# Two moves in an attention phase: half of the stacks' transfers to ScalarE's queue, and the adaptive sums at twice the pace

## The chip, the cores and the metric

The kernel runs on one core of a Trainium2 chip. Its time is the device time of one execution in microseconds. Five engines work side by side, each on its own queue in order: TensorE (PE, with its weight loads shown as PEld), VectorE (DVE), ScalarE (ACT), GpSimd (POOL) and SyncE (SP), which here does nothing but issue transfers. A transfer is issued by an instruction in the queue of an engine (SPq or ACTq in the rows) and is then carried out by the core's 16 DMA engines.

## The reference

Two layers over 512 positions of width 1024. Each layer has a mixer and a gated convolution MLP, each behind an RMS norm that is scaled and shifted by a vector `mod = silu(c) @ w_ada[l] + b_ada[l]` of 6 x 1024 numbers.

```python
def reference(x, c, ...):
    for l in range(DEPTH):
        mod = jax.nn.silu(c) @ w_ada[l] + b_ada[l]
        sh_a, sc_a, gt_a, sh_f, sc_f, gt_f = [...split(mod, 6)]
        h = rms_norm(x, g_attn[l]) * (1.0 + sc_a) + sh_a
        x = x + gt_a * hybrid_mixer(h, ...)
        h = rms_norm(x, g_ffn[l]) * (1.0 + sc_f) + sh_f
        x = x + gt_f * conv_glu_ffn(h, ...)
    return rms_norm(x, g_final)
```

The mixer projects `h` to queries, keys and values of 16 heads and joins three kinds of attention: 4 differential heads (two softmaxes subtracted), 6 dilated heads (three sliding windows with strides), and 6 neighbourhood heads, in which a position of the 8 x 64 grid sees 8 rows and 16 columns around it, with a bias per offset. Their outputs go through `w_out`.

## The kernel before, in words

Everything is fp32 made of two reduced parts: each operand is split in `hi` and `lo`, and each product is three matmuls (L487 to L489, or L760 to L762 for values). Weights come in units of up to 512 KB: `emit_raw` (L333) issues the load into one of four `raw` buffers, `emit_split` casts it to `hi` on ScalarE (L355) and subtracts on VectorE or GpSimd to get `lo` (L357).

The numbers of `mod` are made by 96 **adaptive sums**. `ada_step` (L406) takes one 512 KB piece of `w_ada` from a `raw` buffer, multiplies it with `silu(c)` and adds up on VectorE (L416), and then issues the load of the next piece on SP's queue (`ada_load`, L403). So one piece is loaded ahead, and it takes one of the four `raw` buffers that the weights use too. Sixteen sums are made before the first projection, 24 in the attention phase of layer 0, and the other 56 in its MLP. Layer 1 makes none.

`attention_phase` writes out the order of the work by hand. A loop makes one pass after another (`nst` counts them). In a pass the generator `proj()` emits a piece of the projections, `ck.step()` emits the stages of earlier heads that are due, a stack may be emitted, then an adaptive sum may be, and then at most one new attention step. Step `si` counts 16 differential steps (0 to 15), 24 dilated ones (16 to 39; `NDB` is 40) and 12 of the neighbourhood heads (40 to 51). A credit that grows by 1 a pass, up to 0.5, pays for them: 2 for a differential step, 1.5 for a dilated and 1.7 for a neighbourhood step. The order is the same in both layers but for the sums.

In layer 0 a sum is emitted in each fourth pass from step 10 on. What is left of the 24 when the loop ends is emitted right behind it (L1202), ahead of the output projection, its norm and the MLP.

A **stack** is the arrangement of one pair of heads' keys and queries that lets one matmul multiply `hi` and `lo` together. For neighbourhood pairs `na_stack` (L833) copies from the four tiles `natc` to the tiles `ks`, `qs` and `ql`: 12 transfers of 128 KB, all in SBUF, four lines of code (L841, L842, L844, L845). There are three such stacks in each layer, emitted at steps 32, 40 and 44. The tiles `ks`, `qs` and `ql` have two buffers each, so each stack waits for the last score matmul of the stack two before. Between the first and the second stack the values of the neighbourhood heads go to DRAM and come back in another arrangement, in 4 + 4 transfers of 384 KB (`scv<-va`, L868; `va<-scv`, L871).

On the other side of the loop, a dilated step is: score matmuls (L1036, L1037), a masked maximum on VectorE (L1040), exponential (L1045) and scaling (L1050) on ScalarE, transposes on TensorE (L909), the cast of these to `ph` on ScalarE (L913) and the subtraction to `pl` on VectorE (L917), and the product with the values (L930, L932). A neighbourhood step goes the same way (L1078, L1089, L1101, L1107, L1116, L1118, L1122, L1133). The transposes write PSUM tiles `pt`, of which there are two.

Of the kernel before, what the change touches and what calls it, by code (L numbers as in the profile page):

```python
# [176 lines left out]
def build(ctx, tc, a):  # L177
    nc = tc.nc
    V, A, G, PE, SY = nc.vector, nc.scalar, nc.gpsimd, nc.tensor, nc.sync
# [212 lines left out]
    ada_st = {"n": 0}  # L392
# [13 lines left out]
    def ada_step():  # L406
        if ada_st["n"] >= len(ada_list):
            return
        if not ada_raw:
            ada_load()  # L410
        l, j = ada_list[ada_st["n"]]
        cv = cx if ada_st["n"] < 16 else cb
        r = ada_raw.pop(0)
        ada_st["n"] += 1
        junk = tmp((128, D), BF16)
        V.tensor_tensor_reduce(out=junk, in0=r, in1=cv, op0=ALU.mult, op1=ALU.add, scale=1.0,  # L416
                               scalar=par[:, OFF_B + l * 48 + j:OFF_B + l * 48 + j + 1],
                               accum_out=mod[l][:, j:j + 1])
        g, k = divmod(j, 8)
        if g in (1, 4):  # L420
            o = 0 if g == 1 else 8
            base = OFF_GA if g == 1 else OFF_GF
            g = par[:, base + l * 8 + k:base + l * 8 + k + 1]
            A.activation(out=gsc[l][:, o + k:o + k + 1], in_=mod[l][:, j:j + 1], func=AF.Identity, scale=g, bias=g)
        if ada_st["n"] >= 16 or ada_st["n"] + len(ada_raw) < 16 and l == 0:
            ada_load()
# [213 lines left out]
    def attention_phase(l, gen, fest):  # L640
# [8 lines left out]
        def at(shape, dt, tag, bufs):  # L649
            return ap.tile(list(shape), dt, tag=tag, bufs=bufs, name=f"{tag}{uid()}")  # L650

        def mark(lag, *keys):
            ck.after(lag, lambda: ready.update(keys))
# [179 lines left out]
        def na_stack(p):  # L833
            qh, ql, kh, kl = [t.bitcast(F32) for t in natc[p]]
            K = at([128, 2, S], F32R, "ks", 2)
            Q = at([128, 2, S], F32R, "qs", 2)
            L = at([128, 2, S], F32R, "ql", 2)
            Kf, Qf, Lf = K.bitcast(F32), Q.bitcast(F32), L.bitcast(F32)
            for i in range(2):
                rows = slice(64 * i, 64 * i + 64)  # L840
                SY.dma_start(Kf[0:64, i], kh[rows])  # L841
                SY.dma_start(Kf[64:128, i], kl[rows])  # L842
                for half in range(2):
                    SY.dma_start(Qf[64 * half:64 * half + 64, i], qh[rows])  # L844
                    SY.dma_start(Lf[64 * half:64 * half + 64, i], ql[rows])  # L845
            av["nat"] += 4
            stk["c", p] = (K, Q, L)
            mark(2, ("c", p))
# [211 lines left out]
        def nab_load(hd):  # L1060
            b = at([128, 384], F32, "nab", 2)
            SY.dma_start(b, a["nab"][l, hd])
            nab[hd] = b
# [90 lines left out]
        NDB = 4 * HD + 4 * HB  # L1154
# [17 lines left out]
        for p, at_step in enumerate((NDB - 8, NDB, NDB + 4)):  # L1172
            stacks.append((("natc", p), at_step, lambda p=p: na_stack(p)))
# [6 lines left out]
        credit, si, alive, nst = 0.0, 0, True, 0  # L1180
        while alive or si < len(steps) or ck.heap:
            if alive and next(pg, "end") == "end":
                alive = False
            nst += 1
            assert nst < 2000, (si, av, ready)
            ck.step()
            if stacks and stacks[0][0] in ready and si >= stacks[0][1]:
                stacks.pop(0)[2]()
            if si >= NDB - 8 and not nab:
                nab_load(0)  # L1190
                nab_load(1)
            if l == 0 and ada_st["n"] < 40 and nst % 4 == 0 and si >= 10:
                ada_step()
            credit = min(credit + 1.0, 0.5)
            if si < len(steps) and not ck.held:
                per, need, keys, fn = steps[si]
                if credit >= 0 and all(k in ready for k in keys) and all(av[t] >= n for t, n in need.items()):
                    fn()
                    credit -= per
                    si += 1  # L1200
# [174 lines left out]
    for l in range(DEPTH):  # L1375
        oT = attention_phase(l, rb0, fest)
        norm, rb0, fest = ffn_phase(l, oT)
# [64 lines left out]
```

## Time and profile before

| what | value |
|---|---|
| median of 3 runs | 1357.06 us (1354.73 to 1357.70) |
| profiled execution, its own time | 1349.55 us |
| its span | 1347.8 us |
| TensorE busy | 1285.7 us, 95% of the span |
| VectorE busy | 849.0 us, 63% |
| ScalarE busy | 639.8 us, 47% |
| GpSimd busy | 240.0 us, 18% |
| transfers issued from SP's queue | q1, 203.72 MB |
| transfers issued from ScalarE's queue | q10, 2.39 MB |

The profile is of one execution and was faster than the median of the timed runs. Issuing a transfer and waiting for a semaphore are not counted as busy time of an engine.

### The profile page before, as it was taken

What the parts mean: (1) busy time and instruction counts of PE and PEld (TensorE: products, weight loads), DVE (VectorE), ACT (ScalarE), POOL (GpSimd) and SP (SyncE); (2) the same over time, 40 slices, a digit from 0 to 9 for tenths busy, and PEclk for the clock granted to TensorE, in tenths of its full rate; (3) what the DMA queues carried; (4) which work ended last, traced back from release to release, by engine and by line L of the source; (5) the groups of instructions that cost most, each with busy time, mean ns of one, the idle gap of its engine ahead of it and who ended that gap; (6) DMA issues with size and microseconds to landing.
All of it is one profiled execution on the core that took longest, in us unless ns stands there. A gap on an engine that the chain in (4) does not pass through costs nothing.

```text
span 1347.8 us, 18449 instructions
## 1 busy us (share of the span) xinstructions
PE 1285.7 (95%) x6836; PEld 1102.7 (82%) x6836; DVE 849.0 (63%) x1534; ACT 639.8 (47%) x1150; POOL 240.0 (18%) x163
## 2 busy tenths in 40 slices
PE   5988899899999999999999989999999999999997
PEld 4877698778988888888899868987898888888886
DVE  5659777788676566656674786576775434443443
ACT  4546688665533233323342667887554313331331
POOL 2644522133000000000124344212400000000002
PEclk9999999998999999999999999999999999999999
DMA  9676667853466656665524755472433332333211
GB/s 361 232 207 168 187 199 220 233 161 118 148 204 187 201 175 187 199 191 168 173 77 132 189 156 167 121 212 81 125 118 102 94 94 94 94 94 99 86 36 63
DMA packets 75001, 207.28 MB, mean 154 GB/s; under 512 B 8608, under 2 KB 12576, under 8 KB 74784
## 3 DMA queue, kind: packets, MB, share of 16 engines
q1 hardware_dynamic: 74048, 203.72, 50.4%
q10 hardware_dynamic: 864, 2.39, 0.5%
q8 instruction: 54, 0.88, 0.3%
q14 instruction: 35, 0.29, 0.1%
HBM read 180.91 MB, written 15.73 MB: 146 GB/s over the span
## 4 chain that ended last, share of the span: by engine, by line
PE 72%; DMA 9%; DVE 7%; POOL 4%; issue 4%; ACT 3%; SPq 1%; POOLq 0%; DVEq 0%; ACTq 0%
PE pr L489 9%; PE pr L488 9%; PE pr L487 9%; PE s L488 5%; PE s L487 5%; PE s L489 5%; PE pt L488 4%; PE pt L489 4%; PE pt L487 4%; PE o L488 2%; PE o L489 2%; PE o L487 2%; PE pt L909 2%; DMA raw<-w 1%; PE pr L567 1%
## 5 line engine op out<-in xcount | busy, mean ns | idle before, releaser
L355 ACT CAST whi<-raw 128x1024 fp32r<-128x1024 f32 (+2 forms) x136 | 128.1, 943 | 229.6 <-PE pr L489 78.2
L357 POOL TENSOR_TENSOR wlo<-raw,whi 128x768 fp32r<-128x768 f32 (+2 forms) x58 | 115.0, 1988 | 299.4 <-ACT whi L355 275.4
L448 POOL TENSOR_TENSOR tmp<-tmp,tmp 128x256 f32<-128x256 f32 (+1 forms) x38 | 37.0, 976 | 714.3 <-ACT tmp L446 713.5
L357 DVE TENSOR_TENSOR wlo<-raw,whi 128x1024 fp32r<-128x1024 f32 (+1 forms) x78 | 90.8, 1164 | 101.4 <-ACT whi L355 100.6
L416 DVE CUSTOM_DVE_ANT_0 tmp<-raw,cb,par 128x1024 bf16<-128x1024 f32 x80 | 109.4, 1368 | 52.7 <-DMA raw<-w_ada 52.3
L355 ACT CAST fhi<-raw 128x1024 fp32r<-128x1024 f32 (+1 forms) x76 | 74.6, 985 | 130.6 <-PE pr L489 52.8
L357 DVE TENSOR_TENSOR flo<-raw,fhi 128x1024 fp32r<-128x1024 f32 (+1 forms) x74 | 86.9, 1175 | 56.8 <-ACT fhi L355 56.0
L487 PE MATMUL pr<-h,whi 128*128 128x512 f32 (+1 forms) x300 | 113.2, 378 | 0.4 <-DVE tmp L669 0.4
L489 PE MATMUL pr<-h,whi 128*128 128x512 f32 (+1 forms) x300 | 111.5, 372 | 0.4 <-DVE h L483 0.4
L488 PE MATMUL pr<-h,wlo 128*128 128x512 f32 (+1 forms) x300 | 111.7, 372 | 0.0
L487 PE MATMUL pr<-h,fhi 128*128 128x512 f32 (+1 forms) x244 | 86.8, 358 | 0.1
L488 PE MATMUL pr<-h,flo 128*128 128x512 f32 (+1 forms) x244 | 86.5, 356 | 0.0
L489 PE MATMUL pr<-h,fhi 128*128 128x512 f32 (+1 forms) x244 | 85.8, 358 | 0.3 <-DVE h L483 0.3
L917 DVE TENSOR_TENSOR pl<-pt,ph 128x512 fp32r<-128x512 f32 x80 | 54.6, 685 | 18.0 <-ACT ph L913 17.7
L1267 ACT ACTIVATE tmp<-tmp 128x512 f32<-128x512 f32 x44 | 27.6, 631 | 77.7 <-DVE tmp L1262 77.7
L489 PEld LDWEIGHTS pr<-h,whi 128*128 128x128 f32 x300 | 56.7, 189 | 9.5 <-DVE h L483 0.6
L487 PEld LDWEIGHTS pr<-h,whi 128*128 128x128 f32 x300 | 56.8, 189 | 8.9 <-DVE tmp L669 0.7
L488 PEld LDWEIGHTS pr<-h,wlo 128*128 128x128 f32 x300 | 56.9, 190 | 8.7 <-POOL wlo L357 0.6
L913 ACT CAST ph<-pt 128x512 fp32r<-128x512 f32 x80 | 46.5, 582 | 26.2 <-PE pt L909 25.9
L1003 DVE TENSOR_REDUCE sm<-s 128x1 f32<-128x512 f32 x64 | 42.9, 681 | 25.3 <-PE s L1001 25.0
L909 PE MATMUL pt<-cst,tmp 128*128 128x128 f32 x320 | 48.7, 275 | 9.9 <-DVE tmp L1019 7.0
L909 PEld LDWEIGHTS pt<-cst,tmp 128*128 128x128 f32 x320 | 37.7, 140 | 19.8 <-issue 5.9
(287 smaller groups left out, 3704.9 us busy)
## 6 DMA issues: line engine op xcount, KB each, us to landing
raw<-w SPq DMA_DIRECT2D x132, 512.0 KB
raw<-w_ada SPq DMA_DIRECT2D x80, 512.0 KB
raw<-w SPq DMA_DIRECT2D x64, 384.0 KB
araw<-w_ada SPq DMA_DIRECT2D x16, 512.0 KB
raw<-w SPq DMA_DIRECT2D x16, 320.0 KB
graw<-w SPq DMA_DIRECT2D x8, 384.0 KB
scr0b<-nat SPq DMA_DIRECT2D x12, 256.0 KB
qs<-nat SPq DMA_DIRECT2D x24, 128.0 KB
```

Of the source, the lines that this page charges most:

```text
L355: A.copy(hi, r)
L357: (G if on_pool else V).tensor_tensor(out=lo, in0=r, in1=hi.bitcast(F32), op=ALU.subtract)
L416: V.tensor_tensor_reduce(out=junk, in0=r, in1=cv, op0=ALU.mult, op1=ALU.add, scale=1.0, scalar=par[:, OFF_B + l * 48 + j:OFF_B + l * 48 + ...
L448: self.last = self.eng.tensor_tensor(out=self.sq[0][:, sl], in0=self.sq[0][:, sl], in1=self.sq[m][:, sl], op=ALU.add)
L487: PE.matmul(out, wh, hh, start=first, stop=False)
L488: PE.matmul(out, wl, hh, start=False, stop=False)
L489: return PE.matmul(out, wh, hl, start=False, stop=last)
L909: PE.transpose(pt[:, kt], P[:, kt * 128:kt * 128 + 128], ident)
L913: A.copy(st["ph", half][:, :, sl], pt)
L917: V.tensor_tensor(out=st["pl", half][:, :, sl], in0=st["pt", qb], in1=st["ph", half][:, :, sl].bitcast(F32), op=ALU.subtract)
L1003: V.tensor_reduce(out=nm[:, m:m + 1], in_=s, axis=AX.X, op=ALU.max, negate=True)
L1267: A.activation(out=t, in_=t, func=AF.Silu)
```

## The change

In `na_stack` the six transfers of the pair's second head are issued from ScalarE's queue instead of SP's. The adaptive sums of layer 0's attention are emitted in each second pass instead of each fourth, from step 10 on, and only while `si` is under `NDB - 9`, which is 31. The loop behind the attention, which emits what is left of the 24, stays as it was.

```diff
             for i in range(2):
                 rows = slice(64 * i, 64 * i + 64)
-                SY.dma_start(Kf[0:64, i], kh[rows])
-                SY.dma_start(Kf[64:128, i], kl[rows])
+                E = A if i else SY
+                E.dma_start(Kf[0:64, i], kh[rows])
+                E.dma_start(Kf[64:128, i], kl[rows])
                 for half in range(2):
-                    SY.dma_start(Qf[64 * half:64 * half + 64, i], qh[rows])
-                    SY.dma_start(Lf[64 * half:64 * half + 64, i], ql[rows])
+                    E.dma_start(Qf[64 * half:64 * half + 64, i], qh[rows])
+                    E.dma_start(Lf[64 * half:64 * half + 64, i], ql[rows])
...
-            if l == 0 and ada_st["n"] < 40 and nst % 4 == 0 and si >= 10:
+            if l == 0 and nst % 2 == 0 and 10 <= si < NDB - 9 and ada_st["n"] < 40:
                 ada_step()
```

## Rows read from the trace of the kernel before

**Rows 1.** The page: busy time by engine; a group's busy us, mean ns, idle before.

```profile
PE 1285.7 (95%) x6836; PEld 1102.7 (82%) x6836; DVE 849.0 (63%) x1534; ACT 639.8 (47%) x1150; POOL 240.0 (18%) x163
...
L917 DVE TENSOR_TENSOR pl<-pt,ph 128x512 fp32r<-128x512 f32 x80 | 54.6, 685 | 18.0 <-ACT ph L913 17.7
```

**Rows 2.** Waits of TensorE, 200 to 350 us: total, times, longest.

```profile
PE s L1078 <- issue: 4.1, 1, 4.1
```

**Rows 3.** SP's queue in order of time, stacks of layer 1: start, duration.

```profile
862.07 0.51 SPq L844 DMA_DIRECT2D qs<-nat  x1
...
869.35 0.47 SPq L845 DMA_DIRECT2D ql<-nat  x1
...
881.11 2.73 SPq L871 DMA_DIRECT2D va<-scv  x4
886.27 0.52 SPq L844 DMA_DIRECT2D qs<-nat  x1
...
889.77 0.46 SPq L845 DMA_DIRECT2D ql<-nat  x1
893.94 0.46 SPq L841 DMA_DIRECT2D ks<-nat  x1
896.57 0.46 SPq L842 DMA_DIRECT2D ks<-nat  x1
...
899.36 0.59 SPq L845 DMA_DIRECT2D ql<-nat  x1
```

**Rows 4.** SP's queue, second stack of layer 0: first and last issue of twelve.

```profile
227.28 0.52 SPq L841 DMA_DIRECT2D ks<-nat  x1
...
242.42 0.60 SPq L845 DMA_DIRECT2D ql<-nat  x1
```

**Rows 5.** Waits of SP's queue, whole span (first row) and 860 to 915 us.

```profile
SPq L333 <- DMA rope<-rope: 8.6, 1, 8.6
...
SPq L841 <- DMA va<-scv: 3.7, 1, 3.7
```

**Rows 6.** ScalarE and its queue in order of time, layer 0's start and layer 1.

```profile
40.06 0.82 ACT L540 ACTIVATE h<-xt,mod,gsc 128x512 fp32r<-128x512 f32 x1
40.07 0.34 ACTq L236 DMA_DIRECT2D rope<-rope  x1
...
889.74 0.58 ACT L913 CAST ph<-pt 128x512 fp32r<-128x512 f32 x1
```

**Rows 7.** TensorE in order of time, layer 1's second stack.

```profile
893.73 0.60 PE L909 MATMUL pt<-cst,tmp 128*128 128x128 f32 x4
```

**Rows 8.** Busy time by stretch: length, engines (instructions), clock, DMA share, GB/s.

```profile
125.00:151.60 26.60, 24.35 (x134) 20.33 (x132) 23.73 (x44) 15.55 (x32) 14.78 (x8) 1.00 0.64 174
151.60:202.40 50.80, 48.58 (x278) 42.45 (x279) 37.78 (x91) 38.43 (x80) 17.52 (x10) 1.00 0.68 204
...
232.50:291.80 59.30, 53.59 (x304) 44.50 (x302) 47.06 (x137) 43.64 (x113) 13.58 (x8) 0.97 0.70 193
291.80:322.20 30.40, 25.55 (x164) 23.44 (x163) 22.67 (x36) 14.24 (x27) 14.90 (x14) 0.89 0.53 173
...
891.80:946.80 55.00, 52.49 (x304) 45.07 (x302) 39.34 (x121) 42.33 (x109) 13.06 (x8) 0.97 0.48 129
946.80:972.10 25.30, 23.58 (x163) 21.72 (x163) 17.72 (x29) 14.39 (x26) 14.25 (x14) 0.93 0.40 125
```

**Rows 9.** VectorE in order of time, five of the attention's 24 sums.

```profile
124.96 1.28 DVE L416 CUSTOM_DVE_ANT_0 tmp<-raw,cb,par 128x1024 bf16<-128x1024 f32 x1
...
198.71 1.26 DVE L416 CUSTOM_DVE_ANT_0 tmp<-raw,cb,par 128x1024 bf16<-128x1024 f32 x1
...
247.08 1.29 DVE L416 CUSTOM_DVE_ANT_0 tmp<-raw,cb,par 128x1024 bf16<-128x1024 f32 x1 [5.54 <-DMA raw<-w_ada]
...
293.11 1.85 DVE L416 CUSTOM_DVE_ANT_0 tmp<-raw,cb,par 128x1024 bf16<-128x1024 f32 x1 [0.70 <-DMA raw<-w_ada]
...
297.94 1.27 DVE L416 CUSTOM_DVE_ANT_0 tmp<-raw,cb,par 128x1024 bf16<-128x1024 f32 x1
```

## The prediction

> **What bounds the kernel now.** I read the page's engine shares first. TensorE is busy for 95% of the span [rows 1], so a change pays only where it fills a gap of TensorE, and costs wherever it opens one. Second, TensorE's waits in the stretch where both edits work. The largest is 4.1 us before a score matmul [rows 2], the eight others are 2.2 us or less, and none names a transfer. So no stack comes late for TensorE, and the stacks' speed is worth nothing by itself. Third, SP's queue in order of time, for what the stacks wait for and how long they take to issue. Fourth, the order of ScalarE and TensorE beside the same stacks, for how much slack ScalarE has. Fifth, busy time by stretch, layer 0 beside layer 1: the same matmuls (304 and 304, 164 and 163), but only layer 0 has adaptive sums. From the first neighbourhood score matmul to the last product with the values layer 0 takes 59.3 us and layer 1 55.0, and from there to the second norm 30.4 and 25.3 [rows 8]. The difference, 4.3 + 5.1 = 9.4 us, is what the sums cost in these stretches now.
>
> **The stacks.** Nothing is added or taken away; 6 of 12 issues move from SP to ScalarE, in three stacks of two layers, 36 issues in all. On SP one issue takes its turn every 0.64 us or so: the first stack of layer 1 runs from 862.07 to 869.82 us, almost without a stop [rows 3]. SP gains 36 x 0.64 = 23 us that nothing on TensorE waits for, so that gain counts as nothing. At most the next weight load or bias load, queued behind the stack, goes out 3.8 us sooner.
>
> *What a moved issue brings along.* The second stack shows it. Its first five issues go out from 886.27 on, and then the sixth starts at 889.77, the seventh at 893.94 and the eighth at 896.57 [rows 3]. They wait for `va<-scv` [rows 5], although `ks<-nat` neither reads nor writes what that transfer moves. Counting issues back from the sixth, seventh and eighth gives the second, third and fourth of the four `va<-scv` in each case: eight places. So a transfer is issued only when the one eight places earlier has landed. That this count runs across queues is seen at the start: a weight load on SP waited 8.6 us for the table `rope`, which ScalarE's queue had issued and which the load doesn't touch [rows 5, 6]. So I take it that ScalarE's issues will hold such places too. In the order of the code they are the seventh to twelfth of a stack. In the second stack the seventh and eighth then wait for the third and fourth `va<-scv`, and the ninth to twelfth for SP's first four of the same stack. On SP such a wait blocks only loads. On ScalarE it blocks, in order, all that stands behind it: casts of weights (L355), the cast of a projection (L820), exponentials (L1045), scalings (L1050), casts of the transposes (L913). TensorE's transposes wait for those, and VectorE's `pl` too.
>
> *Second stack.* ScalarE would reach its six issues at about 886.3, when SP reached the stack, since both wait for the same score matmul, and be through when the twelfth is out: 899.36 + 0.59 = 899.95. It is held 13.7 us. How long does TensorE go on? Its transposes at 893.73 need a `pt` buffer, which the cast L913 of 889.74 to 890.32 and a subtraction of 0.69 us on VectorE free [rows 1, 6, 7]: slack 893.73 - 890.32 - 0.69 = 2.7 us. Loss 13.7 - 2.7 = 11.0 us, in each layer: 22. In layer 0 the stack took 227.28 to 243.02, 15.7 us [rows 4], partly behind loads of sums that will be gone there, so I keep 13.7. At 95% busy [rows 1] TensorE has next to no idle time in which to win that back.
>
> *First and third stacks.* There is no such row in the way; ScalarE is held for its own six issues at least, 6 x 0.64 = 3.8 us, and at most for the whole stack of before, 7.75 us [rows 3]. The ninth must wait until the first has landed. I take 5.2 between the two, less the same slack of 2.7: 2.5 a stack, and 10 for the four.
>
> Stacks together: 22 + 10 = 32 us. Below: nothing, if an issue costs ScalarE no time, as `rope`'s went out at 40.07 while L540 ran from 40.06 [rows 6]. Issue time alone would give 6 x (3.8 - 2.7) = 6.6. Above: (15.7 - 2.7) + 11.0 + 4 x (7.75 - 2.7) = 44.
>
> The Trainium skill, DMA: Bandwidth & Descriptors, section "Issuing engines are not separate DMA queues", says that transfers issued from different engines end on the same 16 DMA engines and that a second issuing engine only saves issue time. By that rule the stacks' edit could give back no more than SP's 23 us, which the rows show to be off the path; it would stand at 0 in the sum, and the sum at 5 us. The rule says nothing of a cost on the engine that issues, which is where the rows put it.
>
> **The sums.** Of before's 24, nine are emitted up to step 31, from 124.96 to 198.71 us [rows 9]: passes 32 to 64. A pass is (198.71 - 124.96) / 32 = 2.3 us. At each second pass from 30 to 64 that is 18. The window then shuts, so six are left, and they go to the loop behind the attention, which emitted three before. So they aren't all ahead of the neighbourhood heads.
>
> - Differential steps (125 to 151.6 us): seven sums instead of three. A sum is 1.28 us and 0.08 for the readout, 4 x 1.36 = 5.4 us more. VectorE is busy 23.73 of 26.6 there [rows 8], so at least 5.4 - 2.9 = 2.5 doesn't fit: 2.5 to 5.4, I take 3.
> - Dilated steps (151.6 to 202.4): eleven instead of six, 6.8 us more, in 13.0 us of idle VectorE [rows 8]. What is late is a load: one piece ahead and a sum each 4.6 us, while a load that SP reached late held VectorE for 5.54 us [rows 9]. 0 to 6.8; I take 2.
> - Neighbourhood steps: eight sums gone, with the 5.54 us wait. It can give back what layer 0 is behind layer 1, 4.3 us; I take 4, and nothing is the other end.
> - Behind the attention: four sums started after 291.8 and cost 5.1 us, 1.3 each; now there are six, none with its load ahead but the first. Two more at 1.3 are 2.6. Above, three more in the loop at the spacing of 293.11 to 297.94 [rows 9], 4.8 each, are 14.5, with the weight loads of the MLP queued behind them on SP. I take 4, near the measured price.
>
> Sums together: 3 + 2 - 4 + 4 = +5 us, from -2 (2.5 + 0 - 4.3 + 0) to +27 (5.4 + 6.8 + 0 + 14.5).
>
> **Sum.** 32 + 5 = 37 us, on the profiled execution's 1349.55 us (span 1347.8): 1386.6. The median of the runs shown lies 7.5 us higher, so 1357.06 + 37 = 1394 us.
>
> **The rivals.**
> *Issue time alone.* ScalarE's issues land in its queue where the places eight back are long free, or count for ScalarE alone. For it: the six of a stack need not follow SP's in the final order. Against it: the 8.6 us across the queues. 6.6 + 5 = +12: 1369 us.
> *Faster.* The same place, ScalarE's queue: if it is held for less than the 2.7 us of slack at each stack, the stacks cost nothing, and the sums' removal gives what layer 0 is behind layer 1, 9.4 us: 1348 us. For it: the issue under L540 [rows 6], and idle VectorE among the dilated steps to take the sums. Against it: six times 0.64 is already over 2.7, and six sums still end behind the loop.
> *Heavier.* Layer 0 holds ScalarE the full 15.7 us, the other stacks for 7.75, and the loads of the six last sums come one by one at 4.8 us: 44 + 10 = +54: 1411 us. For it: the shared `raw` buffers. Against it: the loads of sums leave the stretch of the stacks.
>
> **How the numbers follow.** My forecast has 0.62, issue time alone 0.20, faster 0.11, heavier 0.07. About 0.2% (2.7 us) is what a measurement of this kernel tells from no change. Faster takes the third rival, 0.11; within 0.2% gets 0.05, from the lower end of issue time alone; slower has the rest, 0.84. The forecast's own range is 1378 to 1407. To hold 8 in 10 the range reaches to the issue time alone and to the heavier case, 1360 to 1410; it leaves out the faster rival and half of the heavier.
>
> **What would show it.** Right: ACTq rows of `ks<-nat`, `qs<-nat` and `ql<-nat` spread over some 13 us at each second stack, with ScalarE idle between them and TensorE idle from about 7 us after their start; TensorE waiting for ACT L913 or L1118 there, in both layers; layer 1, which has no sums, longer by some 15 us. Wrong: the six ACTq issues within 4 us, ScalarE busy beside them, and layer 1 as long as before; then the step from SP's waits to ScalarE's is the one that failed. For the sums: 18 before the last dilated steps, six behind the loop, VectorE without idle time from 125 to 152 us, and neighbourhood steps of layer 0 without a wait for `raw<-w_ada`.

## The result, and the profile after

The changed kernel takes 1390.24 us (median of 4 runs, 1389.29 to 1391.26) against 1355.89 us for the kernel before beside it: a ratio of 1.0273, with an interval of 1.0252 to 1.0294. The forecast was 1394 us, 37 us slower; the medians lie 34.4 us apart. Its profiled execution took 1391.26 us.

The page of the kernel after, with the engines' busy time, the granted clock in 40 slices, and the two DMA queues that carry the transfers (q10 is ScalarE's):

```profile
span 1389.5 us, 18432 instructions
...
PE 1298.7 (93%) x6836; PEld 1112.3 (80%) x6836; DVE 844.8 (61%) x1534; ACT 638.8 (46%) x1150; POOL 242.0 (17%) x163
...
PEclk9999799998999999999999999999999999999999
...
q1 hardware_dynamic: 71168, 199.00, 47.5%
q10 hardware_dynamic: 3744, 7.11, 1.8%
```

Every engine does the work of before [rows 1], but TensorE's share falls from 95% to 93%. The span is 41.7 us longer than that of before's profiled execution, whose 1349.55 us lie 6.3 under the median. TensorE's busy time rose from 1285.7 to 1298.7 us with the same 6836 instructions: 13.0 of the 41.7 us are matmuls that ran slower, and 28.7 are gaps. (From line 841 on the new kernel's line numbers are one higher: L909 of before is L910.)

TensorE's two largest waits in the whole span (total, times, longest):

```profile
PE o L931 <- DVE sm L1093: 11.6, 2, 6.8
PE pt L910 <- DVE tmp L1020: 11.0, 6, 4.2
```

The first is that of the two second stacks, and the kernel before doesn't have it. The second has 7.0 us in the kernel before; what is new of it lies in the stretch of the sums, where it grew from 3.1 us (86.3 to 232.5 us before) to 7.0 (87.5 to 259.7). Each stretch is followed below.

**A second stack.** ScalarE and its queue in order of time, layer 1 of the kernel after:

```profile
923.44 0.47 ACTq L842 DMA_DIRECT2D ks<-nat  x1
...
925.35 0.47 ACTq L843 DMA_DIRECT2D ks<-nat  x1
925.42 0.60 ACT L914 CAST ph<-pt 128x512 fp32r<-128x512 f32 x1
931.23 0.47 ACTq L845 DMA_DIRECT2D qs<-nat  x1
935.83 0.47 ACTq L846 DMA_DIRECT2D ql<-nat  x1
936.34 0.61 ACTq L845 DMA_DIRECT2D qs<-nat  x1
936.99 0.61 ACTq L846 DMA_DIRECT2D ql<-nat  x1
937.64 0.58 ACT L944 COPY tmp<-o 64x512 f32<-64x512 f32 x1 [11.62 <-DMA qs<-nat]
938.25 0.59 ACT L914 CAST ph<-pt 128x512 fp32r<-128x512 f32 x1
```

The six issues take from 923.44 to 937.60 us, where six of them in a row on SP took 0.64 us each [rows 3]. From 926.02 to 937.64 ScalarE computes nothing: 11.62 us. SP's queue beside it shows what for. SP's waits between 880 and 960 us, in the same kernel:

```profile
SPq L845 <- DMA va<-scv: 6.0, 1, 6.0
SPq L846 <- DMA va<-scv: 4.4, 1, 4.4
```

Put in order of time, SP's four `va<-scv` and then the two queues' issues of this stack together, the first four issues of the stack go out at once. The fifth (ScalarE's, 925.35) stands eight places behind the first `va<-scv`; ScalarE computes up to there, so no wait shows. The sixth (SP's L846, 928.75) stands eight behind the second and waits 4.4 us, the seventh (ScalarE's, 931.23) eight behind the third, the eighth (SP's L845, 935.25) eight behind the fourth and waits 6.0 us. That is the count of eight places that the prediction read from SP's queue and from `rope`, here over both queues at once.

TensorE in order of time, same stretch:

```profile
931.96 0.28 PE L1080 MATMUL s<-ks,ql 128*128 128x256 f32 x1
939.09 1.19 PE L931 MATMUL o<-ph,vb 128*128 128x256 f32 x4 [6.85 <-DVE sm L1093]
```

The name in the brackets is VectorE's, but L931 doesn't read what L1093 writes, and VectorE is not at fault. Its order of time for the same moment:

```profile
938.26 0.68 DVE L947 TENSOR_TENSOR of<-o,tmp 64x512 f32<-64x512 f32 x1 [8.62 <-ACT tmp L944]
938.87 0.15 DVE L1093 TENSOR_SCALAR sm<-sm 128x2 f32<-128x2 f32 x1
```

L931 needs two things, and both stand behind ScalarE's issues. One is the tile `o`, of which there is a single buffer: ScalarE's copy L944 reads it, VectorE's L947 waits 8.62 us for that copy, and only then, at 938.94, is `o` free. The other is `ph`, which ScalarE's cast L914 behind the copy finishes at 938.84. So the held queue reaches TensorE on two ways, directly and through VectorE, 0.1 us apart. In layer 0 ScalarE is held 9.31 us and TensorE waits 4.79.

**The sums.** They land as forecast: 18 from 123.98 to 227.94 us, six from 320.25 to 336.33, behind the loop. What was not forecast is VectorE waiting for their loads. VectorE in order of time among the dilated steps of the kernel after:

```profile
192.46 0.17 DVE L1050 RECIPROCAL sm<-sm 128x1 f32<-128x1 f32 x1 [0.23 <-ACT tmp L1046]
199.93 1.28 DVE L416 CUSTOM_DVE_ANT_0 tmp<-raw,cb,par 128x1024 bf16<-128x1024 f32 x1 [7.30 <-DMA raw<-w_ada]
...
201.13 0.69 DVE L918 TENSOR_TENSOR pl<-pt,ph 128x512 fp32r<-128x512 f32 x1
```

TensorE in the same stretch, and its busy time before and behind the gap (columns as in rows 8):

```profile
196.84 0.63 PE L931 MATMUL o<-ph,vb 128*128 128x256 f32 x4
201.88 1.23 PE L933 MATMUL o<-pl,vb 128*128 128x256 f32 x4 [4.41 <-DVE pl L918]
...
185.00:197.40 12.40, 12.39 (x70) 10.22 (x68) 7.33 (x20) 10.61 (x22) 5.83 (x3) 1.00 0.59 210
201.90:206.00 4.10, 4.10 (x14) 3.62 (x15) 4.10 (x11) 3.49 (x8) 0.00 (x0) 0.50 0.90 294
```

One sum stands 7.30 us for its piece of weights, the subtraction L918 stands behind the sum, and TensorE is idle for 4.41 us. And when TensorE comes back, four matmuls of 256 columns take 1.23 us where they had taken 0.63: the granted clock was 1.00 ahead of the gap and is 0.50 behind it. From 120 to 205 us VectorE waits for a load four times, 13.9 us in all. Busy time by stretch, from further off:

```profile
140.00:154.00 14.00, 13.50 (x56) 11.18 (x57) 6.83 (x13) 5.03 (x10) 7.55 (x6) 0.80 0.32 106
154.00:167.70 13.70, 7.20 (x38) 5.59 (x36) 12.79 (x23) 6.19 (x14) 2.34 (x1) 0.81 0.55 187
167.70:180.00 12.30, 11.56 (x53) 9.29 (x51) 8.72 (x21) 7.36 (x15) 5.58 (x4) 0.79 0.67 176
...
259.70:319.80 60.10, 53.33 (x304) 45.11 (x301) 38.87 (x122) 43.57 (x112) 13.41 (x8) 0.97 0.44 120
319.80:354.50 34.70, 27.02 (x164) 24.70 (x164) 22.85 (x39) 14.54 (x28) 16.67 (x14) 0.85 0.47 158
```

In the first three rows the granted clock is about 0.80 on average, and TensorE is busy for 32.3 of 40.0 us; before, from 125 to 202.4 us, the clock was 1.00 and TensorE busy for 72.9 of 77.4 [rows 8].

The second of these rows is not a wait for a load. VectorE is busy there for 12.79 of 13.70 us, 0.59 us of the rest is for a piece, and TensorE waits for work of VectorE's, three sums among it (at 153.48, 157.53 and 164.05 us). TensorE, VectorE's row just ahead, and the same matmuls of both kernels (first differential to first neighbourhood score matmul, the kernel before last):

```profile
162.00 0.63 PE L910 MATMUL pt<-cst,tmp 128*128 128x128 f32 x4 [4.19 <-DVE tmp L1020]
...
152.80 0.69 DVE L1004 TENSOR_REDUCE sm<-s 128x1 f32<-128x512 f32 x1 [5.10 <-PE s L1002]
...
87.50:259.70 172.20, 146.54 (x768) 123.42 (x766) 122.75 (x263) 106.88 (x225) 50.08 (x26) 0.92 0.66 189
...
86.30:232.50 146.20, 135.84 (x768) 116.22 (x767) 119.06 (x253) 106.78 (x226) 50.23 (x26) 1.00 0.71 198
```

From 147.79 to 152.54 us TensorE makes 20 matmuls of the projections in a row, VectorE stands 5.10 us for a score, and then the scores come close together and VectorE is behind. In the kernel before, TensorE makes no more than 11 such matmuls in a row between 100 and 170 us. So the new pace also changed the order in which TensorE's queue holds its work: the order of the queues is laid down when the kernel is built, and it is not the order of the code.

SP's queue in order of time, around that stretch:

```profile
138.61 0.33 SPq L333 DMA_DIRECT2D raw<-w  x1
153.67 0.81 SPq L403 DMA_DIRECT2D raw<-w_ada  x2
```

For 15 us SP issues nothing: the load of a sum (L403) waits up to 14.6 us for a buffer that GpSimd's L357 must give back, and every weight load stands behind it. In the kernel before, the longest such wait between 120 and 235 us was 7.3 us.

### The profile page after: what moved, and what is told of

It reads as the page before. It is cut to its first block, busy times and chain, and to the rows that moved or that the text cites. A ratio compares the mean times of both kernels' runs of the same rounds, so it can differ in the third digit from the quotient of the medians.

```text
span 1389.5 us, 18432 instructions
## 1 busy us (share of the span) xinstructions
PE 1298.7 (93%) x6836; PEld 1112.3 (80%) x6836; DVE 844.8 (61%) x1534; ACT 638.8 (46%) x1150; POOL 242.0 (17%) x163
## 4 chain that ended last, share of the span: by engine, by line
PE 69%; DMA 10%; issue 6%; DVE 6%; POOL 5%; ACT 3%; SPq 0%; ACTq 0%; POOLq 0%; DVEq 0%
PE pr L489 9%; PE pr L487 9%; PE pr L488 9%; PE s L488 5%; PE s L487 5%; PE s L489 5%; PE pt L488 4%; PE pt L487 4%; PE pt L489 4%; DMA raw<-w_ada 2%; POOL wlo L357 2%; PE o L489 2%; PE o L487 2%; PE o L488 2%; DMA raw<-w 1%
## 5 line engine op out<-in xcount | busy, mean ns | idle before, releaser
L357 POOL TENSOR_TENSOR wlo<-raw,whi 128x768 fp32r<-128x768 f32 (+2 forms) x58 | 116.4, 2011 | 334.7 <-ACT whi L355 321.6
L357 DVE TENSOR_TENSOR wlo<-raw,whi 128x1024 fp32r<-128x1024 f32 (+1 forms) x78 | 90.2, 1157 | 101.9 <-ACT whi L355 101.2
L416 DVE CUSTOM_DVE_ANT_0 tmp<-raw,cb,par 128x1024 bf16<-128x1024 f32 x80 | 105.6, 1320 | 59.0 <-DMA raw<-w_ada 58.5
L357 DVE TENSOR_TENSOR flo<-raw,fhi 128x1024 fp32r<-128x1024 f32 (+1 forms) x74 | 86.9, 1176 | 57.0 <-ACT fhi L355 56.2
L487 PE MATMUL pr<-h,whi 128*128 128x512 f32 (+1 forms) x300 | 115.6, 386 | 2.9 <-DVE tmp L669 2.8
L489 PE MATMUL pr<-h,whi 128*128 128x512 f32 (+1 forms) x300 | 113.8, 380 | 0.4 <-DVE h L483 0.4
L918 DVE TENSOR_TENSOR pl<-pt,ph 128x512 fp32r<-128x512 f32 x80 | 54.8, 686 | 26.0 <-ACT ph L914 25.7
L487 PEld LDWEIGHTS pr<-h,whi 128*128 128x128 f32 x300 | 58.5, 195 | 12.9 <-DVE tmp L669 3.9
L489 PEld LDWEIGHTS pr<-h,whi 128*128 128x128 f32 x300 | 58.0, 193 | 10.1 <-DVE h L483 0.6
L910 PE MATMUL pt<-cst,tmp 128*128 128x128 f32 x320 | 50.9, 284 | 14.3 <-DVE tmp L1020 11.0
L1004 DVE TENSOR_REDUCE sm<-s 128x1 f32<-128x512 f32 x64 | 43.0, 681 | 32.3 <-PE s L1002 32.2
L914 ACT CAST ph<-pt 128x512 fp32r<-128x512 f32 x80 | 46.8, 585 | 28.6 <-PE pt L910 28.1
L910 PEld LDWEIGHTS pt<-cst,tmp 128*128 128x128 f32 x320 | 39.4, 146 | 23.7 <-issue 11.9
```

The source lines that it names most:

```text
L357: (G if on_pool else V).tensor_tensor(out=lo, in0=r, in1=hi.bitcast(F32), op=ALU.subtract)
L487: PE.matmul(out, wh, hh, start=first, stop=False)
L489: return PE.matmul(out, wh, hl, start=False, stop=last)
L910: PE.transpose(pt[:, kt], P[:, kt * 128:kt * 128 + 128], ident)
L914: A.copy(st["ph", half][:, :, sl], pt)
L918: V.tensor_tensor(out=st["pl", half][:, :, sl], in0=st["pt", qb], in1=st["ph", half][:, :, sl].bitcast(F32), op=ALU.subtract)
```

## The experiments

Each was timed in five rounds against the kernel before. A cost in microseconds is the ratio less one, times the median of the kernel before in that call (1353.75, 1352.76 or 1353.13 us).

### The two halves of the change, each alone

Stacks alone:

```diff
-                SY.dma_start(Kf[0:64, i], kh[rows])
...
+                E = A if i else SY
+                E.dma_start(Kf[0:64, i], kh[rows])
...
```

> The stacks' part alone; the sums at their old pace. The prediction's own split gives +32 us over the kernel before (+22 from the second stacks, +10 from the others). The rival split, read from the changed kernel's trace, where layer 1 has no sums and its attention is 7.3 us longer, gives twice that, +15 us, and leaves the rest to the sums. If a moved issue cost nothing but its own issue time, +7 us; if it cost nothing, within 3 us.

Sums alone:

```diff
-            if l == 0 and ada_st["n"] < 40 and nst % 4 == 0 and si >= 10:
+            if l == 0 and nst % 2 == 0 and 10 <= si < NDB - 9 and ada_st["n"] < 40:
```

> The sums' part alone; all stacks issued by SP. The prediction's split gives +5 us (range -2 to +27). The rival split, read from the changed kernel's trace, gives about +20 us, nearly all of it between 124 and 232 us of layer 0, where VectorE waits for late loads of sums; layer 1 is then as long as before.

Stacks alone: 1366.6 us, ratio 1.0088 [1.0071, 1.0105], 11.9 us. Sums alone: 1377.28 us, 1.0167 [1.0149, 1.0184], 22.6 us. Together 34.5; the whole change, by the same measure, is 37.0 (34.2 to 39.9 by its interval). The difference is within the noise, so no effect of the one on the other is seen. But the larger share is the other one: 32 and 5 were expected.

The sums' kernel says where its part lies. From the first differential score matmul to the first neighbourhood one takes 168.3 us there (88.2 to 256.5) against 146.2 before (86.3 to 232.5): 22 us, where the forecast had 3 + 2. The neighbourhood heads take 4.5 us less, where the forecast had 4. The stretch behind them takes 4.7 more up to the first transposes of the norm (L457) and 2.7 more up to the second, where the prediction's stretch ends [rows 8]; the forecast had 4. The lengths of single executions scatter by some us, so these are consistent with the forecast, no more than that.

### The stacks: the second alone, and the others alone

The next three edits are shown against the kernel with the stacks alone.

```diff
-                E = A if i else SY
+                E = A if i and p == 1 else SY
```

> Only the second stack of each layer has its half on ScalarE's queue. If waits for transfers eight places back hold ScalarE there, this is two thirds or more of what all three stacks cost: +22 us by the prediction's split, +10 us by the one read from the changed kernel. If issue time is what costs, it is one third: +2 to +5 us.

```diff
-                E = A if i else SY
+                E = A if i and p != 1 else SY
```

> Only the first and third stacks of each layer have their half on ScalarE's queue, so twice as many issues move as with the second stacks alone. If waits for transfers eight places back are the cost: +10 us by the prediction's split, +5 us by the one read from the changed kernel, less than the second stacks alone in either. If issue time is the cost, twice what the second stacks alone cost.

The second stacks alone, 12 issues moved: 1362.55 us, 1.0063 [1.0042, 1.0084], 8.5 us. The others alone, 24 issues moved: 1358.32 us, 1.0037 [1.002, 1.0054], 5.0 us. An issue moved at the second stack costs 0.71 us, one of the others 0.21, so the price is not the time of an issue but what happens at the second stack. (The two intervals overlap, 5.7 to 11.4 and 2.7 to 7.3 us, but twice as many issues don't cost twice as much.) Per stack it is 4.3 us where the forecast had 11.0, and 1.25 where it had 2.5. Of the 5.0 us, too, a part is such a wait: at the third stack of layer 1 ScalarE is held 7.43 us, and TensorE waits up to 3.1 for the cast behind it.

Why it is less is seen beside the second stack of layer 1 in the kernel with that stack alone, on ScalarE:

```profile
895.61 0.49 ACTq L842 DMA_DIRECT2D ks<-nat  x1
...
897.43 0.59 ACT L914 CAST ph<-pt 128x512 fp32r<-128x512 f32 x1
901.99 0.47 ACTq L843 DMA_DIRECT2D ks<-nat  x1
...
908.38 0.61 ACTq L846 DMA_DIRECT2D ql<-nat  x1
909.02 0.58 ACT L944 COPY tmp<-o 64x512 f32<-64x512 f32 x1 [11.00 <-DMA qs<-nat]
```

and on TensorE:

```profile
904.05 0.28 PE L1080 MATMUL s<-ks,ql 128*128 128x256 f32 x1
910.47 0.98 PE L931 MATMUL o<-ph,vb 128*128 128x256 f32 x3 [6.13 <-DVE sm L1093]
```

ScalarE still computes between its first issue and its second, up to a cast that ends at 898.02, so it is held 11.00 us and not 13.7. And TensorE goes on until 904.33, 6.3 us longer, with projections, scores and transposes whose inputs are ready; the forecast had read 2.7 us of slack from one transpose. The gap is 6.13 us.

### Which half of a stack is moved, and a later second stack

```diff
-                E = A if i else SY
+                E = SY if i else A
```

> The stacks' part alone, but with the halves swapped: ScalarE's queue issues the first six transfers of each stack and SP the last six. The issues moved are as many. If what costs is the wait for the transfer eight places back, the two or three issues behind the last values' returns, and those behind the stack's own first four, now stand on SP, and ScalarE is held some 3 to 5 us at the second stack instead of 11 to 13: +0 to +5 us over the kernel before instead of +12. If the issue time is what costs, +12 us as with the other half.

1367.78 us, 1.0104 [1.0086, 1.0123], 14.1 us: no fall. ScalarE's copy behind the second stack of layer 1 there:

```profile
914.19 0.58 ACT L944 COPY tmp<-o 64x512 f32<-64x512 f32 x1 [10.72 <-DMA qs<-nat]
```

It is held as long as with the other half (10.65 us there). The trace shows why: in the final order the two queues' issues alternate (SP at 900.01 and 900.88, ScalarE 900.89, SP 901.45, ScalarE 902.80), whichever half the code names first. So this edit doesn't tell the theories apart.

The second stack was then put three steps later, once with ScalarE's issues for it (as in the kernel with the second stack alone) and, as a control, with SP's:

```diff
-        for p, at_step in enumerate((NDB - 8, NDB, NDB + 4)):
+        for p, at_step in enumerate((NDB - 8, NDB + 3, NDB + 4)):
```

> Only the second stack has its half on ScalarE's queue, and the stack is emitted three steps later (at step 43 instead of 40), so that the values' returns, eight places back, have landed or nearly so. To be held against the next run. If the wait for those returns is what holds ScalarE, it is held 3 to 6 us instead of 11, and the difference between the two runs is 0 to 3 us instead of the 8.5 us at step 40. If not, it stays at 8.

> The kernel before with the second stack emitted at step 43, all of it issued by SP. The control for the run before it. Within 3 us of the kernel before, or a few us slower where the stack now comes late for step 44.

With ScalarE's issues 1362.4 us, 1.007 [1.0053, 1.0088]; with SP's 1353.9, 1.0007 [0.9993, 1.0022]. The difference is 8.5 us, as much as at the old place. But the issues hardly moved: in layer 1 SP's first goes out at 895.11 us, still directly behind the four `va<-scv` of 890.07. ScalarE is held 8.38 us there, where 3 to 6 had been expected, and TensorE's gaps at the two second stacks are 7.1 and 5.3 us. The wait itself was not taken away, so the test is not the one that was meant. It gives one useful row, ScalarE in layer 0:

```profile
244.28 0.39 ACT L424 ACTIVATE gsc<-mod,par 128x1 f32<-128x1 f32 x1 [6.69 <-DMA va<-scv]
```

Here the profile itself names the transfer that held ScalarE: `va<-scv`, which SP issued and L424 doesn't read. No run here has the second stack's issues on ScalarE without the four transfers ahead of them; that the cost would then be gone is not shown.

### The sums without their loads

In the kernel with the changed pace, and in one with the old pace, the attention's 24 sums read a tile that is in SBUF anyway, and their loads are left out (so these kernels leave out that part of the reference).

```diff
+        skip = 16 <= ada_st["n"] < 40
-        if not ada_raw:
+        if not ada_raw and not skip:
...
-        r = ada_raw.pop(0)
+        r = cb if skip else ada_raw.pop(0)
...
-        if ada_st["n"] >= 16 or ada_st["n"] + len(ada_raw) < 16 and l == 0:
+        if ada_st["n"] >= 40 or ada_st["n"] + len(ada_raw) < 16 and l == 0:
```

> The sums at the changed pace, but the 24 of the attention read the tile of silu(c) in place of their piece of w_ada, so their 24 loads are left out and the sums are not those of the reference; VectorE's work is the same. To be held against the next run. If the +23 us of the sums come from VectorE's queue being held by late loads, the difference between the two is 6 us or less (VectorE's own 1.36 us a sum among the differential steps, less what is gained behind). If they come from VectorE's work alone, it stays near +20.

> The kernel before with the same 24 loads left out (the sums read the tile of silu(c), so they are not those of the reference), at the old pace. The control. 5 to 10 us faster than the kernel before, by the 9.4 us that layer 0 is behind layer 1 in the neighbourhood heads and behind the loop.

Changed pace: 1355.22 us, 1.0008 [0.9994, 1.0023]. Old pace: 1350.33 us, 0.9979 [0.9966, 0.9991]. VectorE has the same sums, emitted at the same passes, as in the kernel with the sums alone, and the pace costs 3.9 us (1.0008 less 0.9979) and not 22.6. So some 19 of the 22.6 us hang on the loads. Not all of that need be waiting on the chip: without the loads the order of TensorE's queue is another one, too. At the old pace they cost 2.8 us; 5 to 10 had been expected.

### The sums with a buffer of their own

If a load waits because it takes turns with the weights in four `raw` buffers, a buffer for the sums alone (and three for the weights) should help.

```diff
-            r = wp.tile([128, n], F32, tag="raw", bufs=4, name=f"raw{uid()}")
+            r = wp.tile([128, n], F32, tag="raw", bufs=3, name=f"raw{uid()}")
...
-            r = wp.tile([128, D], F32, tag="raw", bufs=4, name=f"raw{uid()}")
+            r = wp.tile([128, D], F32, tag="sraw", bufs=1, name=f"raw{uid()}")
```

> The sums' part alone, with a buffer of their own for the pieces of the sums (one) and three raw buffers for the weights, instead of four shared by both. If the +23 us of the sums come from loads that wait for a raw buffer that a weight's split has still to free, most of it goes: +8 us or less over the kernel before. If they come from VectorE having too much to do between 124 and 170 us, it stays at +18 to +25.

> The kernel before with the same split of the buffers (one for the pieces of the sums, three for the weights) and the old pace. The control for the run before it. As before with one piece held at nearly all times, so within 3 us of it; if the shared buffers already delay the sums at the old pace, up to 4 us faster.

Changed pace: 1399.39 us, 1.0337 [1.0312, 1.0362]. Old pace: 1374.76 us, 1.0167 [1.0144, 1.019]. Over the kernel before they cost 45.6 and 22.6 us. At most 8 had been expected of the first, or 18 to 25 if VectorE's work were the cause, and within 3 of the second, so all of these were missed. Between the two it is 23, as with the shared buffers. Waits from 120 to 240 us in the kernel with the sums alone:

```profile
DVE tmp L416 <- DMA raw<-w_ada: 12.8, 6, 6.3
...
SPq L403 <- POOL wlo L357: 30.7, 5, 15.0
```

and in the one with a buffer of their own:

```profile
DVE tmp L416 <- DMA raw<-w_ada: 21.7, 10, 5.1
...
SPq L403 <- DMA raw<-w_ada: 26.7, 10, 5.3
SPq L403 <- DVE mod L416: 25.0, 13, 4.2
```

The wait of a sum's load for GpSimd is gone and two others stand in its place: with one buffer a load must wait until the sum before is through. VectorE waits for its pieces longer than before. The theory that the shared buffers alone make the cost has fallen; what stays in both kernels is a load that is late for its sum.

### Sums earlier at the old pace

```diff
-            if l == 0 and ada_st["n"] < 40 and nst % 4 == 0 and si >= 10:
+            if l == 0 and ada_st["n"] < 40 and nst % 4 == 0 and si >= 2:
```

> The kernel before, with the sums in each fourth pass from step 2 on instead of step 10, so that the last three, which were emitted behind the loop, come inside it. If the three sums behind the loop cost what the tail shows (5.1 us for four there), 2 to 5 us faster. If the differential steps have no room on VectorE for four more sums, same or slower by up to 5 us.

1355.89 us, 1.0026 [1.0008, 1.0044], 3.5 us slower. The first sum is at 93.4 us and the last at 298.63, where before it was from 124.96 to 303.46. Drawing the sums forward gains nothing at the old pace either. No kernel with the reference's whole work beat the one before.

## Why the prediction was right, and where it was not

The sign and the size were right: 37 forecast, 34.4 between the medians and 37.0 by the ratio. The size is partly luck, because two terms were mis-sized in opposite directions: the stacks were taken at 32 us and measure 11.9, the sums at 5 and measure 22.6.

**Stacks.** *No gain.* Right: the transfers are issued from two queues and nothing on TensorE gains by it; this part by itself costs 11.9 us. The Trainium skill, DMA: Bandwidth & Descriptors, section "Issuing engines are not separate DMA queues", bounds what a second issuing engine saves by the issue time. The run agrees as to the gain; on the cost to the engine that issues the section says nothing, and that cost decided here.
*The wait of eight places, taken over by ScalarE.* Right, in both layers: held 11.62 us in layer 1 and 9.31 in layer 0, with `va<-scv` named for SP in the same stretch and for ScalarE in the later second stack. The rival of issue time alone has the stacks at 6.6 us; moving 24 issues for 5.0 us and 12 for 8.5 speaks against it.
*Second stack, 13.7 - 2.7 = 11.0 us.* Too large: it measures 4.3. Held 11.0 and not 13.7; the larger error is the slack, which was read from the first instruction of TensorE that needs ScalarE, a transpose, while TensorE's queue held other matmuls that were ready: 6.3 us and not 2.7. The trace's gap is 6.13 us in layer 1. That 4.3 is less than this gap is consistent with slack won back later: in the one profile of that kernel the neighbourhood heads take 5.7 and 5.9 us longer than before and layer 0's stretch behind them 3.4 less. No run isolates it.
*First and third stacks, 2.5 each.* Also too large: 1.25.
*What waits.* The forecast named TensorE behind ACT L913 or L1118. The row names VectorE's L1093; what L931 needs is the cast (L914, the forecast's L913), done at 938.84, and the tile `o`, free at 938.94. So the forecast named one of two ways that end together, and missed the one through VectorE.

**Sums.** *Where they land.* Right: 18 and six.
*Differential and dilated steps, 3 + 2 us.* This is the step that failed: 22 us, above its own upper ends, 5.4 + 6.8 = 12.2. It costed VectorE's time to sum, and without loads the whole change of pace costs 3.9 us, near the forecast's 5. What it left at "0 to 6.8" was the load: 18 loads of 512 KB in a stretch where nine went out before, on a queue whose other loads wait too. The row of 5.54 us for one late load stood in the prediction [rows 9], and it was taken for an exception; at twice the pace it came four times in the 13 sums of 120 to 205 us, 13.9 us in all. "VectorE without idle time from 125 to 152 us" is wrong as well: it is busy for 6.83 of 14.00 us from 140 on, where it waits 5.10 us for TensorE's scores. That TensorE's queue would be laid down in another order was no term either; its largest gap in that stretch beside the 4.41 us, 4.19 us, stands behind a VectorE that is busy and not waiting.
*The clock.* No term had it. 13.0 of the 41.7 us of span are slower matmuls. 10.7 of them lie between the first differential and the first neighbourhood score matmul of layer 0: 146.5 us busy instead of 135.8 for the same 768 matmuls, at a granted clock of 0.92 instead of 1.00.
*Neighbourhood steps and behind the loop, -4 and +4.* -4.5, and +2.7 over the prediction's own stretch, in the kernel with the sums alone; both within what single executions scatter. In the kernel after, the neighbourhood steps of layer 0 take 60.1 us in spite of it, since the second stack's gap lies there.

Open: which of four things makes the loads cost some 19 us, since they come together: VectorE standing in its order for a piece, SP standing for a buffer with the weight loads behind it, the transfers' share of the DMA engines, or the other order in which the queues are laid down. The buffer of its own took away one form of SP's wait and put another in its place, so it doesn't separate them. A load two pieces ahead was not tried.

## What to carry to other kernels

Before an issue is moved to a compute engine, look at what the issues around it wait for on the queue where they stand: that wait moves along, and on a compute engine it stops everything behind it, and what that feeds. When work is drawn together, cost its loads at the new pace, and ask of one late load in the trace how often it will come at that pace. Look at the order of the queues in the changed kernel's trace, too: an edit can move work that it doesn't name. And split a forecast that comes out right: two wrong terms can make a right sum.

## What was not expected

- Weights with three `raw` buffers in place of four, and one for the sums, cost together, at the old pace, 22.6 us (1374.76 us, 1.0167 [1.0144, 1.019]): as much as the sums at twice the pace.
- An idle stretch is paid twice. After the gaps of 4.41 and 6.85 us the next matmuls of 4 x 256 columns took 1.23 and 1.19 us, against 0.63 just before the first of them. The granted clock is 0.50 in the 4 us behind either gap, 1.2 in place of 2.4 GHz.
